# Opening a hybrid decoder block: first four FFN products accumulated side by side, a decay-rate row loaded whole, three small-piece loads issued from GpSimd

## The chip, the core and the metric

The kernel runs on one core of a Trainium2 chip. A core has TensorE (PE in the profile, PEld for its weight loads), VectorE (DVE), ScalarE (ACT), GpSimd (POOL) and SyncE (SP), which work in parallel, each through its own instructions in order, and 16 DMA engines. The metric is the device time of one execution in microseconds (us), lower is better.

## The reference, cut to what matters

One layer of a decoder trunk on 512 tokens of width 1024, all in float32. First comes half a SwiGLU FFN; then three mixing branches (a state-space branch, a dilated attention, a cross-attention); then a second FFN.

```python
def rmsnorm(x, g):
    y = xf * lax.rsqrt(jnp.mean(xf * xf, axis=-1, keepdims=True) + EPS)
    return y * g
def swiglu_ffn(x, w_in, w_down):              # w_in: 1024 x 5632, D_FF = 2816
    a, b = jnp.split(x @ w_in, 2, axis=-1)
    return (jax.nn.silu(a) * b) @ w_down
def s5_scan(u, a_re, a_im, log_dt, b_re, b_im, c_re, c_im, d_skip):
    dt = jnp.exp(log_dt)[:, None]             # 32 groups, 64 states each
    mag = jnp.exp(a_re * dt); ang = a_im * dt # abar = mag * (cos ang, sin ang)
    ...
x = x + 0.5 * swiglu_ffn(rmsnorm(x, ffn1_norm), ffn1_w_in, ffn1_w_down)
u = rmsnorm(x, mix_norm)
...
```

## The kernel before, in words

A tile-level scheduler writes each engine's order of instructions at build time. It simulates the program, takes at each point the ready instruction of highest priority (earliest in the program unless the priority is shifted), and adds the semaphores. On the chip each engine then follows that order: an instruction that waits holds up everything behind it on its engine, and a DMA issue that waits or finds its queue full holds up the later issues of that engine.

**Products.** A float32 product is made of two parts that TensorE takes as fp32r: `split` (lines L124 and L125) writes the rounded part `wh` on ACT and the rest `wl` on DVE, three buffers each. A block of 128 output columns times 512 tokens over 1024 inputs (`mm_T`) is 24 matmuls of 128x512: for each of eight 128-row slices k, `wh` by `uh` (L133), `wh` by `ul` (L134), `wl` by `uh` (L135), all into one PSUM bank of the tag `ps_mm` (four banks). Raw weights come in chunks of 1 MB, 256 columns by 1024 rows, into two buffers `wraw` (L109): a chunk can be loaded when both halves of the chunk that held its buffer have been split.

**The start.** `x` is loaded in four pieces of 256 columns, `xn0` to `xn3` (512 KB each, the first in two halves, L247). TensorE transposes each 128-column slice (L260); ACT and DVE write the split slice `uh`, `ul` scaled by the gain g1 (L139, L140) and an unscaled copy `xT`. GpSimd squares each piece (`sqn`, L270) and DVE reduces it (`ssn`, L271). From the four sums DVE computes `r_nat`, one over the root of the mean square per token (a chain of small `rs_` operations, L149 to L159, L274). `norm_rows` spreads it into the tile `rb`: DVE writes four diagonal tiles `dg` (L231), TensorE multiplies them by ones (L232), DVE copies (L233). As the gain is already in `uh`, `ul`, the row factor is multiplied in behind the product, when PSUM is read (`ff_a`, L297; `ff_b`, L305).

The first two weight chunks of FFN 1, for a and for b, are loaded in four halves of 512 KB (`load_first`, L117), each 128 columns of all 1024 rows: the first behind xn0, the other three behind xn3. Then four products follow one after the other: a of column block 0, b of block 0, a of block 1, b of block 1. Each of them needs all eight slices of x.

**Preparation for the state-space branch** (`ssm_prep`) is written with a lower priority beside FFN 1, so that the scheduler fills gaps with it. It takes `log_dt` (32 numbers, spread over 128 partitions by 16 columns: 2 loads of 1024 single numbers, L410 on SP), computes exp, sine and cosine by small DVE operations (`sm`, L365 to L390), builds tables on GpSimd, and loads `par` (L493), `cn` (L499), `bre` and `bim` (L524, L525: 2048 pieces of 64 bytes each) and `dcol` (L547: 512 single numbers), all on SP. Its tiles come from a pool opened after the pool `start`, which holds xn and sqn, has been closed.

Only the functions around the start, the SSM preparation and FFN 1 are touched.

Of the kernel before, what the change touches and what calls it, by code (L numbers as in the profile page):

```python
# [14 lines left out]
AF = mybir.ActivationFunctionType  # L15
# [69 lines left out]
def kernel(ctx, tc, x, mem, ffn1_norm, ffn1_w_in, ffn1_w_down, mix_norm, w_in, a_re, a_im, log_dt,  # L85
                             b_re, b_im, c_re, c_im, d_skip, w_glu, rel_table, w_up_attn, mem_norm, w_kv, w_up_mem,
                             w_out, ffn2_norm, ffn2_w_in, ffn2_w_down, final_norm, onehot, parity, out):
    nc = tc.nc
    V, S, G, TE = nc.vector, nc.scalar, nc.gpsimd, nc.tensor
# [12 lines left out]
    ident = cpool.tile([P, P], F32, name="ident")  # L102
# [9 lines left out]
    first_raw = {}  # L112
    for c0 in (0, FF):
        first_raw[c0] = wpool.tile([P, KD, 2 * P], F32, name="wraw", tag="wraw", bufs=2)

    def load_first(c0, j):
        nc.sync.dma_start(first_raw[c0][:, :, j * P:(j + 1) * P],  # L117
                          ffn1_w_in[0][:, c0 + j * P:c0 + (j + 1) * P].rearrange("(k p) c -> p k c", p=P))

    def split(raw, eng=V):  # L120
        _, nk, n = raw.shape
        h = wpool.tile([P, nk, n], F32R, name="wh", tag="wh", bufs=3)
        l = wpool.tile([P, nk, n], F32R, name="wl", tag="wl", bufs=3)
        S.activation(h, raw, AF.Copy)  # L124
        eng.tensor_tensor(l, raw, h.bitcast(F32), op=ALU.subtract)  # L125
        return h, l

    def mm_T(ps, w, rhs, first=True, last=True):

        h, l = w  # L130
        n = len(rhs)
        for k in range(n):
            TE.matmul(ps, h[:, k, :], rhs[k][0], start=first and k == 0, stop=False)  # L133
            TE.matmul(ps, h[:, k, :], rhs[k][1], start=False, stop=False)  # L134
            TE.matmul(ps, l[:, k, :], rhs[k][0], start=False, stop=last and k == n - 1)  # L135
# [35 lines left out]
    def ps_tile(tag, bufs=None):  # L171
        return ps["pool"].tile([P, T], F32, name="ps_" + tag, tag="ps_" + tag, bufs=ps["mm"] if tag == "mm" else bufs)
# [6 lines left out]
    g1 = cpool.tile([P, 8], F32, name="g1")  # L179
# [59 lines left out]
    start = ExitStack()  # L239
    sp = start.enter_context(sb_pool("start"))  # L240
    nc.sync.dma_start(g1_in, ffn1_norm[0].rearrange("(k p) -> k p", p=P))
    xn = []
    for c in range(4):
        xc = sp.tile([P, 4, 256], F32, name=f"xn{c}")
        n = 128 if c == 0 else 256
        for h in range(0, 256, n):
            nc.sync.dma_start(xc[:, :, h:h + n], x.rearrange("(j r) d -> j r d", r=4)[:, :, c * 256 + h:c * 256 + h + n])  # L247
        xn.append(xc)
        if c == 0:
            load_first(0, 0)  # L250
    load_first(FF, 0)
    load_first(0, 1)
    load_first(FF, 1)
    pv1 = ps_tile("tr", 2)
    TE.transpose(pv1[:, :8], g1_in, ident[:8, :8])
    V.tensor_copy(g1, pv1[:, :8])
    for k in range(KD):
        pt = ps_tile("mm") if k % 2 or k == 0 else ps_tile("tr", 2)
        for r in range(4):
            TE.transpose(pt[:, r * P:(r + 1) * P], xn[k // 2][:, r, (k % 2) * P:(k % 2 + 1) * P], ident)  # L260
        norm_split(k, pt, g1)
        if k % 2 == 0:
            S.activation(xT[k], pt, AF.Copy)
        else:
            V.tensor_copy(xT[k], pt)
# [11 lines left out]
    U = list(zip(uh, ul))  # L277


    def ffn_in(w, f, pool, g, late_r):  # L280

        if w is ffn1_w_in and f == 0:
            ra, rbk = first_raw[0], first_raw[FF]
        else:
            ra = load_chunk(w[0], 0, KD, f * P, 2 * P)
            rbk = load_chunk(w[0], 0, KD, FF + f * P, 2 * P)
        for j in range(2):
            pa = ps_tile("mm")
            mm_T(pa, split(ra[:, :, j * P:(j + 1) * P]), U)
            if f + j == 0 and late_r:  # L290
                norm_sums()
            pb = ps_tile("mm")
            mm_T(pb, split(rbk[:, :, j * P:(j + 1) * P]), U)
            if f + j == 0:
                norm_rows()
            a = pool.tile([P, T], F32, name="ff_a", tag="ff_a", bufs=2)
            V.tensor_tensor(a, pa, rows["r"], op=ALU.mult)  # L297
            t = pool.tile([P, T], F32, name="ff_t", tag="ff_t", bufs=2)
            S.activation(t, a, AF.Tanh, scale=0.5)
            V.scalar_tensor_tensor(a, t, 1.0, a, op0=ALU.add, op1=ALU.mult)  # L300
            b = pool.tile([P, T], F32, name="ff_b", tag="ff_b", bufs=2)
            if late_r:
                V.tensor_tensor(b, a, pb, op=ALU.mult)  # L303
            else:
                V.tensor_tensor(b, pb, rows["r"], op=ALU.mult)  # L305
                V.tensor_tensor(b, a, b, op=ALU.mult)  # L306
            split_plain(b, *g[f + j])
# [47 lines left out]
    def ssm_prep(pool):  # L355
        cnt = [0]

        def small(dt=F32, shape=(P, 16)):
            cnt[0] += 1
            return pool.tile(list(shape), dt, name=f"sm{cnt[0]}")  # L360
# [44 lines left out]
            return tt(q, exp2i(k2), MUL)  # L405

        are, aim, = vec[:, 32:48], vec[:, 48:64]
        ldt = small()
        for g in range(2):
            nc.sync.dma_start(ldt[64 * g:64 * g + 64, :],  # L410
                                bass.AP(tensor=log_dt.tensor, offset=log_dt.offset + g, ap=[[0, 64], [2, 16]]))
        dt = exp(ldt)
        mag = exp(tt(are, dt, MUL))
        mag2 = tt(mag, mag, MUL)
# [6 lines left out]
        k = round_near(ang, 2.0 / math.pi)  # L421
        r = ang
        for part in PIO2_PARTS:
            r = stt(k, -part, r, MUL, ADD)
        r2 = tt(r, r, MUL)
        q = tsc(r2, 1.0 / math.factorial(9), MUL)
        for n, sg in ((7, -1.0), (5, 1.0), (3, -1.0)):
            q = stt(q, sg / math.factorial(n), r2, ADD, MUL)
        sn = stt(q, 1.0, r, ADD, MUL)
        q = tsc(r2, -1.0 / math.factorial(10), MUL)  # L430
        for n, sg in ((8, 1.0), (6, -1.0), (4, 1.0), (2, -1.0)):
            q = stt(q, sg / math.factorial(n), r2, ADD, MUL)
# [38 lines left out]
        w = 1  # L471
# [23 lines left out]
        for part, src in enumerate((c_re, c_im)):  # L495
            flat = src[0].rearrange("g h p -> (g h) p")
            for i in range(4):
# [6 lines left out]
                pt = ps_tile("tr", 2)  # L504
# [16 lines left out]

        bre = pool.tile([P, 16, 16], F32, name="bre")
        bim = pool.tile([P, 16, 16], F32, name="bim")
        nc.sync.dma_start(bre, b_re[0].rearrange("(q g) p h -> (g p) q h", g=2))  # L524
        nc.sync.dma_start(bim, b_im[0].rearrange("(q g) p h -> (g p) q h", g=2))  # L525
        tmp = pool.tile([P, 16, 16], F32, name="btmp")

        def cscale(b, c, nm):
# [15 lines left out]
            V.memset(dup[part], 0.0)  # L544
        dcol = pool.tile([P, 16], F32, name="dcol")
        V.memset(dcol, 0.0)
        nc.sync.dma_start(dcol[96:, :], d_skip[0].rearrange("(q g) h -> (g h) q", g=2))  # L547
        gs = pool.tile([P, 16, 32], F32, name="gs")
        for i in range(4):
            for part in range(2):  # L550
# [5 lines left out]
                pt = ps_tile("tr", 2)  # L556
# [13 lines left out]
            pt = ps_tile("tr", 2)  # L570
# [617 lines left out]
```

## Time and profile before

| | us |
|---|---|
| median of 3 runs | 1306.02 |
| lowest and highest of the 3 | 1302.16, 1306.84 |
| profiled execution | 1308.34 |
| its span in the trace | 1306.6 |
| TensorE busy | 1266.2 (97%) |
| VectorE busy | 721.0 (55%) |
| ScalarE busy | 417.0 (32%) |
| GpSimd busy | 168.6 (13%) |

The span is what the trace covers of one execution; the 1.7 us between span and profiled time lie around it. A row of the timeline reads: start, time, engine, line, operation, what is written from what, count, and in brackets the idle time before it with what ended it; operations are pipelined, so the start-to-start distance of matmuls is their pace, not the duration. SPq rows are DMA issues on SyncE's queue; their time is that of issuing, not of the transfer. A row of waits reads: who waited for whom, us in total, times, longest. A row of windows reads: stretch, its length, busy time (and instructions) of PE, PEld, DVE, ACT, POOL, granted TensorE clock, DMA share and rate.

### The profile page before, as it was taken

To read this page: it belongs to the slowest core of one execution; us is meant where nothing else is said; L and a number is where in the kernel's file an instruction comes from. 1 tells how busy PE (TensorE), PEld (TensorE's weight loads), DVE (VectorE), ACT (ScalarE), POOL (GpSimd) and SP (SyncE) were. 2 spreads that over 40 slices of the span, in tenths; PEclk is the share of its full clock that TensorE was granted. 3 is DMA by queue.
4 is the path that set the end of the run, shared out by engine and by line. 5 is a ranking of instruction groups with operands and counts; after the bars stand their busy time and mean duration, and the time that the engine had idled before them with its cause. 6 is when DMAs were issued, how large, how long until landed. Compare 5 with 4: busy or idle time off the path is not lost.

```text
span 1306.6 us, 15550 instructions
## 1 busy us (share of the span) xinstructions
PE 1266.2 (97%) x6116; PEld 1039.3 (80%) x6116; DVE 721.0 (55%) x1309; ACT 417.0 (32%) x631; POOL 168.6 (13%) x154
## 2 busy tenths in 40 slices
PE   7598999999999999999999999999999999999997
PEld 5487888778888888998887777888888888888886
DVE  5699555786545847655435555445553444444444
ACT  3222232123323432324433444334233222222223
POOL 2069100440003005230000000001100000000002
PEclk9799999999999999999999999999999999999999
DMA  4421432554525755544217221144423223223231
GB/s 130 114 95 60 166 129 73 138 137 149 167 65 186 234 181 169 164 133 147 81 33 185 65 65 40 61 132 139 129 71 107 95 83 106 91 93 99 95 97 65
DMA packets 161409, 149.34 MB, mean 114 GB/s; under 512 B 34132, under 2 KB 144788, under 8 KB 161044
## 3 DMA queue, kind: packets, MB, share of 16 engines
q1 hardware_dynamic: 137856, 133.75, 33.0%
q10 hardware_dynamic: 23480, 14.59, 3.8%
q8 instruction: 48, 0.79, 0.3%
q14 instruction: 25, 0.20, 0.0%
HBM read 133.35 MB, written 16.16 MB: 114 GB/s over the span
## 4 chain that ended last, share of the span: by engine, by line
PE 87%; DVE 6%; DMA 2%; POOL 2%; SPq 1%; ACT 1%; issue 1%; ACTq 0%; DVEq 0%
PE ps_mm L133 23%; PE ps_mm L135 22%; PE ps_mm L134 22%; PE ps_dn L1096 3%; PE ps_dn L1095 3%; PE ps_dn L1097 3%; DVE wl L125 2%; PE ps_acc L873 1%; PE ps_mm L810 1%; PE ps_mm L811 1%; PE ps_mm L812 1%; PE ps_tr L866 1%; SPq L493 1%; PE ps_acc L721 1%; DMA cn<-in_ssm_c_re_dram 1%
## 5 line engine op out<-in xcount | busy, mean ns | idle before, releaser
L124 ACT ACTIVATE wh<-wraw 128x1024 fp32r<-128x1024 f32 (+2 forms) x238 | 227.6, 958 | 647.5 <-PE ps_mm L134 443.5
L133 PE MATMUL ps_mm<-uh,wh 128*128 128x512 f32 x1056 | 415.3, 394 | 0.5 <-ACT uh L143 0.5
L134 PE MATMUL ps_mm<-ul,wh 128*128 128x512 f32 x1056 | 413.2, 392 | 1.8 <-DVE ul L144 1.8
L135 PE MATMUL ps_mm<-uh,wl 128*128 128x512 f32 x1056 | 414.0, 392 | 0.2 <-DVE wl L125 0.2
L125 DVE TENSOR_TENSOR wl<-wraw,wh 128x1024 fp32r<-128x1024 f32 (+2 forms) x238 | 274.3, 1153 | 176.6 <-ACT wh L124 170.6
L134 PEld LDWEIGHTS ps_mm<-ul,wh 128*128 128x128 f32 x1056 | 199.2, 189 | 43.6 <-DVE ul L144 2.8
L133 PEld LDWEIGHTS ps_mm<-uh,wh 128*128 128x128 f32 x1056 | 199.2, 189 | 42.9 <-ACT uh L143 1.0
L135 PEld LDWEIGHTS ps_mm<-uh,wl 128*128 128x128 f32 x1056 | 199.0, 188 | 43.1 <-issue 0.9
L217 POOL TENSOR_TENSOR sqacc<-sqacc,sqk 128x512 f32<-128x512 f32 x12 | 20.2, 1683 | 476.0 <-ACT sqk L216 476.0
L297 DVE TENSOR_TENSOR ff_a<-ps_mm,rb 128x512 f32<-128x512 f32 x44 | 30.4, 690 | 88.0 <-PE ps_mm L135 87.9
L135 PE MATMUL ps_mm<-gh,wl 128*128 128x512 f32 x176 | 70.6, 403 | 3.3 <-DVE wl L125 3.2
L134 PE MATMUL ps_mm<-gl,wh 128*128 128x512 f32 x176 | 70.7, 402 | 0.0
L133 PE MATMUL ps_mm<-gh,wh 128*128 128x512 f32 x176 | 70.7, 403 | 0.0
L1096 PE MATMUL ps_dn<-wl,gh 128*128 128x512 f32 x176 | 70.2, 399 | 0.0
L1095 PE MATMUL ps_dn<-wh,gh 128*128 128x512 f32 x176 | 69.3, 394 | 0.0
L1097 PE MATMUL ps_dn<-wh,gl 128*128 128x512 f32 x176 | 68.8, 392 | 0.0
L1110 POOL TENSOR_TENSOR x2n<-x2n,fnb 128x512 f32<-128x512 f32 x4 | 5.1, 1296 | 357.1 <-ACT junk L1108 357.1
L303 DVE TENSOR_TENSOR ff_b<-ff_a,ps_mm 128x512 f32<-128x512 f32 x22 | 15.1, 688 | 52.6 <-PE ps_mm L135 52.6
L143 ACT ACTIVATE gh<-ff_b 128x512 fp32r<-128x512 f32 x44 | 27.5, 624 | 50.7 <-DVE ff_b L306 46.3
L135 PEld LDWEIGHTS ps_mm<-gh,wl 128*128 128x128 f32 x176 | 33.4, 190 | 12.5 <-DVE wl L125 4.1
L133 PEld LDWEIGHTS ps_mm<-gh,wh 128*128 128x128 f32 x176 | 33.5, 190 | 8.4 <-issue 0.6
L1095 PEld LDWEIGHTS ps_dn<-wh,gh 128*128 128x128 f32 x176 | 33.0, 188 | 8.6
(318 smaller groups left out, 1663.8 us busy)
## 6 DMA issues: line engine op xcount, KB each, us to landing
wraw<-in_ffn_w_in_dram SPq DMA_DIRECT2D x42, 1024.0 KB, 5.1
wraw<-in_w_in_dram SPq DMA_DIRECT2D x25, 1024.0 KB, 5.4
wraw<-in_ffn_w_down_dram SPq DMA_DIRECT2D x12, 768.0 KB, 4.7
wraw<-in_ffn_w_down_dram SPq DMA_DIRECT2D x8, 1024.0 KB, 5.0
wraw<-in_ffn_w_down_dram SPq DMA_DIRECT2D x10, 512.0 KB, 3.5
wraw<-in_xattn_w_kv_dram SPq DMA_DIRECT2D x4, 1024.0 KB, 6.5
wraw<-in_ssm_w_glu_dram SPq DMA_DIRECT2D x8, 512.0 KB, 7.7
wraw<-in_w_out_dram SPq DMA_DIRECT2D x4, 1024.0 KB, 5.7
```

The costliest lines, as they stand in the source:

```text
L124: S.activation(h, raw, AF.Copy)
L125: eng.tensor_tensor(l, raw, h.bitcast(F32), op=ALU.subtract)
L133: TE.matmul(ps, h[:, k, :], rhs[k][0], start=first and k == 0, stop=False)
L134: TE.matmul(ps, h[:, k, :], rhs[k][1], start=False, stop=False)
L135: TE.matmul(ps, l[:, k, :], rhs[k][0], start=False, stop=last and k == n - 1)
L143: S.activation(h, src, AF.Copy)
L217: (V if k == KD - 1 else G).tensor_tensor(rows["sq"], rows["sq"], sq, op=ALU.add)
L297: V.tensor_tensor(a, pa, rows["r"], op=ALU.mult)
L303: V.tensor_tensor(b, a, pb, op=ALU.mult)
L1095: TE.matmul(pd[r], gh[:, tok], h, start=st, stop=False)
L1096: TE.matmul(pd[r], gh[:, tok], l, start=False, stop=False)
L1097: TE.matmul(pd[r], gl[:, tok], h, start=False, stop=en)
```

## The change

Three edits. First, the first chunks of weights are loaded in eight pieces of 256 KB, each two 128-row slices by 256 columns, two pieces behind each piece of x; and the four first products are accumulated together, in all four `ps_mm` banks: after the two slices of a piece of x are transposed and split, both weight pieces are split and 24 matmuls add those slices to the four products. The transposes get two banks of a new tag `ps_tx` beside the two of `ps_tr`. `ffn_in` at f = 0 then takes the four finished banks. Second, `log_dt` is loaded as one row of 32 numbers repeated on 128 partitions, issued from ACT, and two DVE copies pick the numbers out. Third, the loads of `bre`, `bim` and `dcol` are issued from GpSimd.

```diff
-    def load_first(c0, j):
-        nc.sync.dma_start(first_raw[c0][:, :, j * P:(j + 1) * P],
-                          ffn1_w_in[0][:, c0 + j * P:c0 + (j + 1) * P].rearrange("(k p) c -> p k c", p=P))
+    def load_first(c0, k):
+        nc.sync.dma_start(first_raw[c0][:, k:k + 2, :],
+                          ffn1_w_in[0][k * P:(k + 2) * P, c0:c0 + 2 * P].rearrange("(k p) c -> p k c", p=P))
...
-        if c == 0:
-            load_first(0, 0)
-    load_first(FF, 0)
-    load_first(0, 1)
-    load_first(FF, 1)
+        for c0 in (0, FF):
+            load_first(c0, 2 * c)
...
-    for k in range(KD):
-        pt = ps_tile("mm") if k % 2 or k == 0 else ps_tile("tr", 2)
...
+    first_ps = {(c0, j): ps_tile("mm") for j in range(2) for c0 in (0, FF)}
+    for c in range(4):
+        for k in (2 * c, 2 * c + 1):
+            pt = ps_tile("tx" if k % 2 else "tr", 2)
...
+        for c0 in (0, FF):
+            h, l = split(first_raw[c0][:, 2 * c:2 * c + 2, :])
+            for j in range(2):
+                for i in range(2):
+                    k, cols, o = 2 * c + i, slice(j * P, (j + 1) * P), first_ps[(c0, j)]
+                    TE.matmul(o, h[:, i, cols], uh[k], start=k == 0, stop=False)
+                    TE.matmul(o, h[:, i, cols], ul[k], start=False, stop=False)
+                    TE.matmul(o, l[:, i, cols], uh[k], start=False, stop=k == KD - 1)
...
         for j in range(2):
...
+            if begun:
+                pa, pb = first_ps[(0, j)], first_ps[(FF, j)]
...
-        ldt = small()
+        ldt, ldt_all = small(), small(shape=(P, 32))
+        nc.scalar.dma_start(ldt_all, bass.AP(tensor=log_dt.tensor, offset=log_dt.offset, ap=[[0, P], [1, 32]]))
         for g in range(2):
-            nc.sync.dma_start(ldt[64 * g:64 * g + 64, :],
-                                bass.AP(tensor=log_dt.tensor, offset=log_dt.offset + g, ap=[[0, 64], [2, 16]]))
+            rows = slice(64 * g, 64 * g + 64)
+            V.tensor_copy(ldt[rows], ldt_all[rows].rearrange("p (q g) -> p g q", g=2)[:, g])
...
-        nc.sync.dma_start(bre, b_re[0].rearrange("(q g) p h -> (g p) q h", g=2))
-        nc.sync.dma_start(bim, b_im[0].rearrange("(q g) p h -> (g p) q h", g=2))
+        nc.gpsimd.dma_start(bre, b_re[0].rearrange("(q g) p h -> (g p) q h", g=2))
+        nc.gpsimd.dma_start(bim, b_im[0].rearrange("(q g) p h -> (g p) q h", g=2))
...
-        nc.sync.dma_start(dcol[96:, :], d_skip[0].rearrange("(q g) h -> (g h) q", g=2))
+        nc.gpsimd.dma_start(dcol[96:, :], d_skip[0].rearrange("(q g) h -> (g h) q", g=2))
```

More of the change, by code (lines that the diff above doesn't have):

```diff
@@ L256 @@
     V.tensor_copy(g1, pv1[:, :8])
-    for k in range(KD):
-        pt = ps_tile("mm") if k % 2 or k == 0 else ps_tile("tr", 2)
[L259 to L265, printed above, removed]
+    first_ps = {(c0, j): ps_tile("mm") for j in range(2) for c0 in (0, FF)}
+    for c in range(4):
+        for k in (2 * c, 2 * c + 1):
+            pt = ps_tile("tx" if k % 2 else "tr", 2)
+            for r in range(4):
+                TE.transpose(pt[:, r * P:(r + 1) * P], xn[k // 2][:, r, (k % 2) * P:(k % 2 + 1) * P], ident)
+            norm_split(k, pt, g1)
+            if k % 2 == 0:
+                S.activation(xT[k], pt, AF.Copy)
+            else:
+                V.tensor_copy(xT[k], pt)
+        for c0 in (0, FF):
[6 more added lines that the diff above has]
+                    TE.matmul(o, l[:, i, cols], uh[k], start=False, stop=k == KD - 1)
     ssn = rpool.tile([P, 4, 4], F32, name="ssn")
@@ L280, in ffn_in @@
     def ffn_in(w, f, pool, g, late_r):
-        if w is ffn1_w_in and f == 0:
-            ra, rbk = first_raw[0], first_raw[FF]
-        else:
+        begun = w is ffn1_w_in and f == 0
+        if not begun:
             ra = load_chunk(w[0], 0, KD, f * P, 2 * P)
@@ L287, in ffn_in @@
         for j in range(2):
[L288 to L293, printed above, removed]
+            if begun:
+                pa, pb = first_ps[(0, j)], first_ps[(FF, j)]
+            else:
+                pa = ps_tile("mm")
+                mm_T(pa, split(ra[:, :, j * P:(j + 1) * P]), U)
+                if f + j == 0 and late_r:
+                    norm_sums()
+                pb = ps_tile("mm")
+                mm_T(pb, split(rbk[:, :, j * P:(j + 1) * P]), U)
             if f + j == 0:
```

## The prediction

> **What bounds the kernel now.** I read the page's busy times first, then the waits of TensorE, then busy time by stretches, then the timeline around the largest wait.
>
> ```profile
> span 1306.6 us, 15550 instructions
> PE 1266.2 (97%) x6116; PEld 1039.3 (80%) x6116; DVE 721.0 (55%) x1309; ACT 417.0 (32%) x631; POOL 168.6 (13%) x154
> ...
> PE ps_tr L232 <- DVE dg L231: 14.6, 1, 14.6
> PE ps_tr L260 <- DMA xn<-in_x_dram: 4.3, 1, 4.3
> ...
> 0.00:14.60 14.60, 6.13 (x30) 5.55 (x30) 6.97 (x11) 6.64 (x9) 6.48 (x9) 1.00 0.84 244
> 14.60:31.40 16.80, 16.80 (x79) 13.81 (x77) 10.69 (x19) 6.12 (x9) 2.32 (x2) 1.00 0.19 40
> 31.40:46.30 14.90, 0.30 (x3) 0.01 (x1) 4.02 (x41) 1.06 (x1) 0.00 (x0) 0.61 0.44 92
> 46.30:55.50 9.20, 9.20 (x34) 7.73 (x35) 8.77 (x26) 2.21 (x3) 0.00 (x0) 0.70 0.46 125
> ```
>
> TensorE bounds the kernel (97%), so only its lost time is to be won, and almost all of it lies at the start: no product matmul before 14.6 us, then three products, then 14.6 us of waiting for `dg`, then the fourth product until 55.5. The timeline says why `dg` was late.
>
> ```profile
> 16.91 1.36 SPq L410 DMA_DIRECT2D sm<-in_ssm_log_dt_dram  x2
> 23.45 0.39 SPq L109 DMA_DIRECT2D wraw<-in_ffn_w_in_dram  x1
> 23.88 11.15 SPq L493 DMA_DIRECT2D par<-in_parity_dram  x1
> 24.27 1.02 DVE L544 MEMSET dup<- 128x512 f32 x2
> 40.38 0.18 DVE L367 TENSOR_SCALAR sm<-sm 128x16 f32<-128x16 f32 x1 [14.99 <-DMA sm<-in_ssm_log_dt_dram]
> 44.50 1.06 ACT L124 ACTIVATE wh<-wraw 128x1024 fp32r<-128x1024 f32 x1 [14.16 <-DMA wraw<-in_ffn_w_in_dram]
> 44.84 0.26 DVE L502 TENSOR_SCALAR cd<-cn,par 128x64 f32<-128x64 f32 x1 [1.90 <-DMA cn<-in_ssm_c_re_dram]
> 45.95 0.87 DVE L231 TENSOR_SCALAR dg<-ident,r_nat 128x128 f32<-128x128 f32 x4
> ...
> q1 hardware_dynamic: 653, 0.00, 4.8%
> ```
>
> The last row is the DMA queue from 24 to 30 us: 653 packets, no bytes to speak of, 4.8% of 16 engines. That is `log_dt`, 2,048 single numbers at 6/653 = 9.2 ns each, 18.8 us in all. DVE's order has an operation on it (40.38) ahead of the `rs_` chain, so `r_nat`, `dg` and `norm_rows` wait behind a number that FFN 1 doesn't need. Behind the same pieces stand SP's issue of `par` (11.15 us), the loads of `cn`, and the next weight chunk, issued at 23.45 and landed at 44.5.
>
> **Edit 1: log_dt as one row.** It removes the 2,048 pieces and adds 128 rows of 128 bytes, issued on ACT, and two small DVE copies (an estimate by the 128x16 row above, 0.18 us each). The nearest row for the load is `cn`, also 128 rows, in 1.7 us.
>
> ```profile
> cn<-in_ssm_c_re_dram SPq DMA_DIRECT2D x4, 32.0 KB, 1.7
> bim<-in_ssm_b_im_dram SPq DMA_DIRECT2D x1, 128.0 KB, 8.1
> ...
> q1 hardware_dynamic: 3923, 0.75, 68.8%
> ```
>
> So both stalls go: DVE's 15 us, and SP's queue with what stood in it. What is late next on DVE is `cn`: on SP behind L109, which waits for a split of the first weights (24.7 us by the count below), so `cn` lands near 27 and `dg` is written near 29; needed at 36. ACT's issue stands in ACT's order; what waits behind it are splits that TensorE wants 6 us later. I charge nothing for edit 1's added work; without that cover it is the 1.7 us of a load.
>
> **Edit 2: four products side by side.** I rebuild the start. First the data, from the rows where an engine waited for it.
>
> ```profile
> 4.38 1.97 PE L260 MATMUL ps_mm<-ident,xn 128*128 128x128 f32 x8 [1.67 <-DMA xn<-in_x_dram]
> 9.15 1.06 ACT L124 ACTIVATE wh<-wraw 128x1024 fp32r<-128x1024 f32 x1 [2.08 <-DMA wraw<-in_ffn_w_in_dram]
> 10.68 1.12 PE L260 MATMUL ps_tr<-ident,xn 128*128 128x128 f32 x4 [4.33 <-DMA xn<-in_x_dram]
> 15.49 1.07 ACT L124 ACTIVATE wh<-wraw 128x1024 fp32r<-128x1024 f32 x1 [0.19 <-DMA wraw<-in_ffn_w_in_dram]
> 14.60 0.48 PE L133 MATMUL ps_mm<-uh,wh 128*128 128x512 f32 x1
> 16.98 0.60 PE L260 MATMUL ps_tr<-ident,xn 128*128 128x128 f32 x4
> 54.36 0.39 PE L134 MATMUL ps_mm<-ul,wh 128*128 128x512 f32 x1
> 55.26 0.39 PE L135 MATMUL ps_mm<-uh,wl 128*128 128x512 f32 x1
> 47.30 0.43 PE ps_mm L133
> 52.22 0.23 PE ps_mm L133
> ```
>
> In order of issue, 1.0 MB was there at 9.15, 1.5 MB at 10.7, 3.0 MB at 15.5: 3.2 us per MB. In the new order the first weight piece ends at 0.75 MB, so 8.3 us; the second at 9.15; then x and weights of the four steps are complete at 9.15, 12.3, 15.5 and 18.7. With 0.6 us for the first split (a little over half of the 1.06 row) the first product matmul starts at 9.0 instead of 14.6.
>
> One step is 24 matmuls; the pace is (55.26 - 54.36)/4 = 0.225 us, so 5.4 us. Transposes of the next two slices: four in 0.60 us, so 1.2 per step. A step takes 6.6 us, twice the 3.2 us of its data. Its other engines keep up, by these rows:
>
> ```profile
> L140 DVE SCALAR_TENSOR_TENSOR ul<-ps_mm,g,uh 128x512 fp32r<-128x512 f32 x5 | 3.7, 746 | 3.4 <-ACT uh L139 3.3
> L265 DVE COPY xT<-ps_mm 128x512 f32<-128x512 f32 x4 | 2.7, 681 | 0.0
> L144 DVE TENSOR_TENSOR gl<-ff_b,gh 128x512 fp32r<-128x512 f32 x1 | 0.7, 681 | 0.0
> L271 DVE TENSOR_REDUCE ssn<-sqn 128x4 f32<-128x1024 f32 x4 | 4.8, 1212 | 0.0
> L297 DVE TENSOR_TENSOR ff_a<-ps_mm,rb 128x512 f32<-128x512 f32 x2 | 1.4, 681 | 0.0
> L232 PE MATMUL ps_tr<-dg,ones 128*128 128x128 f32 x8 | 2.3, 440 | 14.6 <-DVE dg L231 14.6
> ```
>
> DVE per step: two `ul` (1.5), one `xT` (0.7), two half-size `wl` (1.4, as `gl`), one `ssn` (1.2), together 4.8 us, less than 6.6. ACT has less still.
>
> The clock at the start: the windows show 1.00, but transposes at 10.68 took 1.12 us for four, at 16.98 only 0.60, and after the long idle the matmuls ran 0.43 us apart from 47.3 until 52 and then 0.23. So TensorE worked at half pace for the 3.9 us from 10.68 to 14.6, and for some 5.5 us after 46.3. The new first step meets this with matmuls instead of transposes: 3.9 to 5.5 us at half pace lose 2.0 to 2.8; I take 2.3, and 0 as the other end, should the early transposes already have set the pace. The Trainium skill, "TensorE: Matmul & The Clock Gate", Part 1, has the idle clock at half and releases it after about 3.4 us of activity; taken alone it would cost 1.7 us here, and it agrees with the pace in these rows and not with the granted clock of 1.00 beside them.
>
> End of the fourth product: 9.0 + 5.4 + 2.3 + 3 x 6.6 = 36.5 us. All four banks are then full, and the next chunk's product needs one: `norm_rows` (8 passes, 2.3 us at half pace, so some 1.0), the copy to `rb` (0.7) and `ff_a` (0.7) come first, 2.4 us; 0 if the scheduler put `norm_rows` earlier. Then 38.9, against 55.6 for the same point before (the fourth product's last matmul at 55.26, and two transposes behind it). **Gain 16.7 us.** The next chunk's weights are not late: their buffer is free when the last a-piece is split, which waits for a `wh` buffer that step 2 gives back at 23.3; split by 24.7, landed 5 us later.
>
> **Edit 3: bre, bim, dcol from GpSimd.** 4,096 pieces of 64 bytes and 512 of 4 leave SP's queue. No GpSimd load is in this trace, so I bound it. Floor: 40 to 46 us moved 3,923 packets at 68.8% of the engines, 1.5 ns a piece, 7 us for all. Ceiling: `log_dt`'s 9.2 ns a piece, 42 us. GpSimd's own rows:
>
> ```profile
> 5.31 1.90 POOL L270 TENSOR_TENSOR sqn<-xn 128x1024 f32<-128x1024 f32 x1 [4.02 <-DMA xn<-in_x_dram]
> 10.70 6.22 POOL L270 TENSOR_TENSOR sqn<-xn 128x1024 f32<-128x1024 f32 x3 [3.50 <-DMA xn<-in_x_dram]
> ...
> POOL cosT L477 <- DVE sm L372: 59.0, 1, 59.0
> ```
>
> Its last `sqn` ends at 16.9 and it then has nothing to do for 59 us, which hides either, provided that the issues stand behind the four `sqn`. I take it that they do: DVE had idle time before 10 us, yet the preparation's first operations (`dup`, 24.27) ran only when x was used up. The floor is nearest, since it is the same loads; cost nothing on the path, 7 us of DMA between 19 and 27 us, where only one 1 MB chunk with 6 us to spare runs.
>
> The Trainium skill, "DMA: Bandwidth & Descriptors", section "Issuing engines are not separate DMA queues", speaks against expecting more of this edit: loads from all engines share the same 16 DMA engines and interleave. No run here shows a GpSimd load; if the loads went out at the start, its rule would give the first rival.
>
> **Behind the start** the preparation overloads DVE and GpSimd:
>
> ```profile
> 126.00:135.00 9.00, 5.82 (x19) 4.37 (x18) 9.00 (x6) 1.48 (x2) 8.24 (x4) 0.81 0.57 188
> ```
>
> TensorE loses 3.2 us there and 0.19 x 9 = 1.7 to the clock. The preparation and FFN 1 both move ahead by about the same time, so I leave it; it can vanish (-5) or grow (+5).
>
> **The sum.** Against the profiled execution: 1308.3 - 16.7 = 1291.6. Its time is 2.3 above the median of 1306.0; against that 1289.3.
>
> **The rivals.**
> - *Early small pieces* (0.15). GpSimd is idle until 5.3 us; if the issues stand ahead of `sqn`, 4,608 pieces take up to 7 us of all DMA engines beside x and the first weights: 1296. For it: nothing that the code orders; against it: the late `dup`.
> - *Another head of line* (0.10). DVE still meets `cn` or the new row late, `rb` misses 36.5 and TensorE idles and cools: 5 to 9 us, so 1294 to 1299.
> - *Given back* (0.08). The scheduler's new order makes the jam at 126 worse, or adds one; twice that jam and a cold restart return some 10 us: 1299 to 1303, within the bound of no change.
> - *Slower* (0.06). One mechanism: GpSimd makes the pieces slowly and ahead of `sqn`. DVE's `ssn` then waits, and behind it the splits that TensorE needs for step 2. The restart is at X + 3, X being GpSimd's hold (one `sqn` and one `ssn`, 1.9 + 1.2), the same point is reached at X + 3 + 19.8 + 2.4; that passes 55.6 from X = 30 us on. At the ceiling of 42 it is 67, a loss of 12: 1318.
> - *It does not do what it says* (0.01): the row lands as late as the pieces; then only the earlier start counts, about 1300.
>
> **How the numbers follow.** The main case has 0.60: 1289.3, own range 1281 (no `norm_rows` wait, -2.4; jam gone, -4.9) to 1295 (jam grows, +5). For 8 in 10 the range reaches from 1280 over the first two rivals to 1299. Half a per cent, 6.5 us, is about what a measurement tells from no change (the three runs spread 4.7). Faster, below 1299.5: 0.60 + 0.15 + 0.09 of the rest = 0.84; same 0.09; slower 0.07.
>
> **What would show it.** Right: first product matmul near 9, matmul pace 0.43 then 0.225, no wait of `dg` over 3 us, the f = 2 products starting near 39, SP's issue of `par` under 1 us. Wrong: `sqn` or `ssn` waiting behind GpSimd's issues; a DVE wait for `cn` or the row past 36 us; the time before the f = 2 products won, and lost again between 60 and 140 us.

## The result, and the profile after

The changed kernel takes 1295.38 us (median; 1293.01 to 1295.93) beside 1306.24 for the kernel before in the same session: a ratio of 0.992, 95% interval 0.9896 to 0.9944. Five more rounds on another chip gave 1293.42 against 1304.86, 0.9915 (0.9901 to 0.993). So it is faster by some 11 us. One execution of a kernel told below, r_row, ran at a granted clock of 0.77 and took 1527.33 us; its ratio leaves that one out. The forecast was 1289.3 with a range of 1280 to 1299: the direction and the range held, and the likeliest value was 6 us too low.

First the head of the page after, and TensorE's waits. A row of waits reads: who waited for whom, us in total, times, longest.

```profile
span 1293.4 us, 15577 instructions
PE 1265.6 (98%) x6116; PEld 1038.5 (80%) x6116; DVE 727.0 (56%) x1315; ACT 417.5 (32%) x635; POOL 169.9 (13%) x157
PE ps_mm L135 <- DVE wl L125: 7.1, 3, 3.8
```

The 14.6 us wait for `dg` is gone and no other has taken its place at the start. On top now stands a wait of the down products (the second half of FFN 1, with `w_down`) for `wl`, 7.1 us in three pieces. In the kernel before the same row read 3.4:

```profile
PE ps_mm L135 <- DVE wl L125: 3.4, 2, 3.2
```

Now the timeline of the start after (start, us, engine, line, what is written from what, count; in brackets the idle time before it).

```profile
8.87 1.22 PE L271 MATMUL ps_mm<-uh,wh 128*128 128x512 f32 x2 [2.60 <-ACT wh L124]
12.88 0.63 PE L272 MATMUL ps_mm<-ul,wh 128*128 128x512 f32 x1
13.30 0.63 PE L271 MATMUL ps_mm<-uh,wh 128*128 128x512 f32 x1
16.35 0.39 PE L271 MATMUL ps_mm<-uh,wh 128*128 128x512 f32 x1
16.58 0.39 PE L272 MATMUL ps_mm<-ul,wh 128*128 128x512 f32 x1
18.30 1.35 POOL L535 DMA_DIRECT2D bre<-in_ssm_b_re_dram  x1
19.65 1.16 POOL L536 DMA_DIRECT2D bim<-in_ssm_b_im_dram  x1
29.35 0.57 SPq L504 DMA_DIRECT2D par<-in_parity_dram  x1
30.91 0.07 DVE L479 MEMSET cosT<- 128x16 f32 x1 [0.84 <-PE ps_tx L260]
31.46 0.38 ACTq L419 DMA_DIRECT2D sm<-in_ssm_log_dt_dram  x1
33.42 1.05 PE L232 MATMUL ps_tr<-dg,ones 128*128 128x128 f32 x8
37.85 0.50 PE L133 MATMUL ps_mm<-uh,wh 128*128 128x512 f32 x1 [0.27 <-DVE ff_a L307]
```

The reader is to see four things. The first product matmul runs at 8.87, and matmuls start 0.42 us apart at 13 and 0.23 apart at 16.4. The transposes by `dg` (`norm_rows`, 33.42) run inside the fourth step, so the second chunk's products (f = 2) start at 37.85 with 0.27 us of waiting. SyncE's issue of `par` fell from 11.15 us to 0.57. And `log_dt` is asked for only at 31.46, just after the memset at 30.91 that had to wait for the last transposes of x.

The place where time was given back is shown by windows of 5 us (stretch, its length, busy time and instructions of PE, PEld, DVE, ACT, POOL, granted clock, DMA share, GB/s).

```profile
105.00:110.00 5.00, 3.70 (x17) 2.68 (x16) 4.96 (x5) 1.36 (x2) 5.00 (x6) 1.00 0.00 0
110.00:115.00 5.00, 3.85 (x17) 2.77 (x15) 4.96 (x5) 0.00 (x0) 5.00 (x4) 1.00 0.51 157
115.00:120.00 5.00, 4.08 (x12) 3.18 (x13) 4.99 (x4) 1.79 (x3) 4.92 (x4) 0.69 0.01 3
120.00:125.00 5.00, 1.92 (x8) 1.25 (x6) 4.97 (x4) 1.15 (x2) 4.84 (x3) 0.97 0.39 159
125.00:130.00 5.00, 4.31 (x13) 3.45 (x14) 5.00 (x5) 0.00 (x0) 2.88 (x1) 0.71 0.77 267
```

TensorE is busy 17.9 of these 25 us, so it idles 7.1, the wait above; DVE is full in all five windows and GpSimd nearly to its last operation. Two stretches also show a granted clock of 0.69 and 0.71: there matmuls start 0.43 us apart instead of 0.23. Before, the same jam (the stretch in which the down products' splits come late) was shorter: 3.2 us idle between 126 and 135.

To measure it in one number for every kernel I take the distance from the first f = 2 matmul to the row of the fourth sum of a down product (`xT`, behind the jam; each sum adds a down product to `xT`). The work between is 361 matmuls in every kernel but x4_dup and r_dup. After, it ends here; the second row is that of before, which started f = 2 at 55.63:

```profile
131.27 0.69 DVE L599 SCALAR_TENSOR_TENSOR xT<-ps_mm,xT 128x512 f32<-128x512 f32 x1 [1.11 <-PE ps_mm L135]
143.88 0.69 DVE L588 SCALAR_TENSOR_TENSOR xT<-ps_mm,xT 128x512 f32<-128x512 f32 x1 [2.28 <-PE ps_mm L135]
```

That is 93.4 us after and 88.25 before. The balance of the two profiled executions: 17.8 us won up to f = 2, 5.2 lost from there to the fourth sum, 0.6 won in the whole rest, together 13.2, which is the difference of the spans (1306.6 and 1293.4). A second profile of the changed kernel (r_after) gives 19.4 won, 8.4 lost, 1.8 won.

The window over the distance says what it is made of; after's reads:

```profile
37.85:131.27 93.42, 86.28 (x361) 69.92 (x362) 89.17 (x231) 24.49 (x33) 56.66 (x66) 0.96 0.30 101
```

TensorE idles 7.1 us of it and is busy 86.3. Without a wait and at full clock it is busy 82.4 for the same matmuls (x5_notab below), so the other 3.9 go to matmuls at half clock. Before had 3.5 us idle and 2.4 at half clock: of the 5.2 us lost, 3.7 are waits and 1.5 the clock.

### The profile page after: what moved, and what is told of

Its sections match the earlier page's. It is cut to its first block, busy times and chain, and to the rows that moved or that the text cites. A ratio compares the mean times of both kernels' runs of the same rounds, so it can differ in the third digit from the quotient of the medians.

```text
span 1293.4 us, 15577 instructions
## 1 busy us (share of the span) xinstructions
PE 1265.6 (98%) x6116; PEld 1038.5 (80%) x6116; DVE 727.0 (56%) x1315; ACT 417.5 (32%) x635; POOL 169.9 (13%) x157
## 4 chain that ended last, share of the span: by engine, by line
PE 86%; DVE 4%; DMA 4%; POOL 4%; ACT 1%; issue 1%; SPq 0%; ACTq 0%; POOLq 0%; DVEq 0%
PE ps_mm L133 22%; PE ps_mm L135 22%; PE ps_mm L134 22%; PE ps_dn L1107 3%; PE ps_dn L1106 3%; PE ps_dn L1108 3%; DMA cad<-ca 2%; DVE wl L125 1%; PE ps_acc L884 1%; PE ps_mm L821 1%; PE ps_mm L823 1%; PE ps_mm L822 1%; PE ps_tr L877 1%; DMA wraw<-in_ffn_w_in_dram 1%; PE ps_acc L732 1%
## 5 line engine op out<-in xcount | busy, mean ns | idle before, releaser
L133 PE MATMUL ps_mm<-uh,wh 128*128 128x512 f32 x1024 | 402.0, 393 | 0.8 <-ACT uh L143 0.6
L134 PE MATMUL ps_mm<-ul,wh 128*128 128x512 f32 x1024 | 399.8, 391 | 1.6 <-DVE ul L144 1.6
L135 PE MATMUL ps_mm<-uh,wl 128*128 128x512 f32 x1024 | 400.3, 391 | 0.0
L125 DVE TENSOR_TENSOR wl<-wraw,wh 128x1024 fp32r<-128x1024 f32 (+2 forms) x242 | 277.3, 1147 | 176.7 <-ACT wh L124 170.6
L133 PEld LDWEIGHTS ps_mm<-uh,wh 128*128 128x128 f32 x1024 | 192.7, 188 | 42.0 <-ACT uh L143 1.0
L134 PEld LDWEIGHTS ps_mm<-ul,wh 128*128 128x128 f32 x1024 | 192.7, 188 | 41.6 <-DVE ul L144 1.9
L135 PEld LDWEIGHTS ps_mm<-uh,wl 128*128 128x128 f32 x1024 | 192.5, 188 | 41.4 <-issue 0.9
L134 PEld LDWEIGHTS ps_mm<-gl,wh 128*128 128x128 f32 x176 | 33.9, 193 | 8.1 <-issue 0.2
```

## The experiments

The experiments tell two explanations apart. **A**: the gain is that of the `log_dt` row; the four products and the GpSimd loads add little at the start, and the longer jam is a consequence of edit 2, which keeps x in use until 30 us and so delays the preparation against FFN 1. **B**: all three edits carry the gain, and the jam grew because DVE got more work or by chance of the new order. One row of the table is one profiled execution; the medians are of the timed runs, and each ratio is to the kernel before in the same session. The last two columns split what the distance has over 82.4 us: TensorE idle, and TensorE busy longer (half clock; in x4_dup and r_dup also nine and four matmuls more, 2.0 and 0.9 us, that ran before the row).

| kernel | median us | ratio to before (95%) | f = 2 starts | first table op | fourth sum | distance | idle | busy longer |
|---|---|---|---|---|---|---|---|---|
| before | 1306.24 | 1 | 55.63 | 75.91 | 143.88 | 88.25 | 3.5 | 2.4 |
| after | 1295.38 | 0.992 (0.9896 to 0.9944) | 37.85 | 69.98 | 131.27 | 93.4 | 7.1 | 3.9 |
| x1_row | 1292.38 | 0.9892 (0.9868 to 0.9916) | 38.90 | 59.39 | 128.57 | 89.7 | 4.0 | 3.3 |
| x2_four | 1311.62 | 1.0042 (1.0029 to 1.0055) | 54.13 | 88.70 | 149.88 | 95.75 | 6.7 | 6.6 |
| x3_sp | 1296.93 | 0.9925 (0.9897 to 0.9953) | 38.60 | 72.33 | 136.07 | 97.5 | 10.8 | 4.2 |
| x4_dup | 1286.76 | 0.9858 (0.9829 to 0.9888) | 37.09 | 69.24 | 126.13 | 89.0 | 2.6 | 4.0 |
| x5_notab | 1281.67 | 0.9813 (0.9799 to 0.9828) | 36.88 | 69.02 | 119.29 | 82.4 | 0 | 0 |
| x6_row_dup | 1291.39 | 0.9884 (0.9868 to 0.9901) | 39.85 | 60.33 | 127.34 | 87.5 | 2.8 | 2.3 |
| x7_trfirst | 1292.39 | 0.9898 (0.9882 to 0.9913) | 40.18 | 60.75 | 129.04 | 88.9 | 4.3 | 2.2 |
| x8_trfirst_dup | 1292.51 | 0.99 (0.9879 to 0.9921) | 39.53 | 61.30 | 128.57 | 89.0 | 3.0 | 3.6 |
| r_after | 1293.42 | 0.9915 (0.9901 to 0.993) | 36.22 | 68.38 | 132.92 | 96.7 | 7.7 | 6.6 |
| r_row | 1291.3 | 0.9893 (0.9878 to 0.9908) | 39.36 | 59.85 | 129.16 | 89.8 | 4.0 | 3.4 |
| r_dup | 1287.61 | 0.9867 (0.9853 to 0.988) | 35.98 | 68.09 | 124.95 | 89.0 | 2.6 | 3.9 |
| x9_late | 1288.88 | 0.9883 (0.9864 to 0.9901) | 37.72 | 69.86 | 120.14 | 82.4 | 0 | 0 |

"First table op" is GpSimd's first operation on the table `cosT`. What lies behind the fourth sum takes 1158.5 to 1164.5 us in these profiled executions whatever the edit; no difference of total time under some 3 us between two kernels is laid to a cause here on the strength of one profile.

### x1_row: before, with log_dt as one row alone

```diff
 # before.py
-            nc.sync.dma_start(ldt[64 * g:64 * g + 64, :], ...)      # single numbers
+        nc.scalar.dma_start(ldt_all, ... ap=[[0, P], [1, 32]])
+            V.tensor_copy(ldt[rows], ldt_all[rows].rearrange("p (q g) -> p g q", g=2)[:, g])
```

> The kernel before with edit 1 alone (log_dt as one row from ACT; products, loads and queues as before). Theory A: the row alone takes away both the wait for dg and the full queue of SP, so the fourth product follows the third without a gap (31.4 + 5.4 us) and the f = 2 products start at 37 to 39 us, as in the changed kernel; then edit 2's earlier start (8.9 instead of 14.6 us) is worth nothing, since the transposes and the half-paced clock only move in between the matmuls. Median 1294 to 1298. Theory B, the prediction's sum: the 5.7 us of earlier start are a part of the gain of their own; f = 2 starts at 42 to 44 and the median is 1299 to 1302.

Measured: 1292.38 us, 0.9892 (0.9868 to 0.9916). The timeline of this kernel:

```profile
17.44 0.39 ACTq L409 DMA_DIRECT2D sm<-in_ssm_log_dt_dram  x1
38.90 0.48 PE L133 MATMUL ps_mm<-uh,wh 128*128 128x512 f32 x1
59.39 0.23 POOL L478 TENSOR_TENSOR cosT<-cosT,sm 128x16 f32<-128x16 f32 x1 [42.32 <-DVE sm L372]
```

The row alone brings f = 2 to 38.90, only 1.05 us behind the full change. It asks for `log_dt` 14 us earlier than after does, its tables start 10.6 us earlier, and its jam is about as before (89.7). It is the whole gain; B falls in its first half. Theory A had f = 2 right and the median 2 us too high.

### x2_four: after, with edits 1 and 3 undone

```diff
 # after.py
-        nc.scalar.dma_start(ldt_all, ...)
-            V.tensor_copy(ldt[rows], ...)
+            nc.sync.dma_start(ldt[64 * g:64 * g + 64, :], ...)      # single numbers
-        nc.gpsimd.dma_start(bre, ...)      # bim, dcol likewise
+        nc.sync.dma_start(bre, ...)
```

> The changed kernel with edits 1 and 3 undone (four products side by side, log_dt as 2,048 single numbers on SP, bre, bim and dcol on SP). Theory A: DVE's order still has an operation on log_dt ahead of the rs_ chain, so rb comes after 40 us, TensorE waits and cools, f = 2 starts at 46 to 52; median 1300 to 1306. Theory B: four banks full of work cover most of the wait, f = 2 starts near 43 and the median is 1296 to 1300.

Measured: 1311.62 us, 1.0042 (1.0029 to 1.0055): slower than before, and than both theories said. Its first wait and its timeline:

```profile
PE ps_tr L515 <- DVE rb L233: 17.0, 1, 17.0
28.42 2.03 SPq L420 DMA_DIRECT2D sm<-in_ssm_log_dt_dram  x2
32.05 1.05 PE L232 MATMUL ps_tr<-dg,ones 128*128 128x128 f32 x8
51.20 0.17 DVE L377 TENSOR_SCALAR sm<-sm 128x16 f32<-128x16 f32 x1 [17.27 <-DMA sm<-in_ssm_log_dt_dram]
52.20 0.68 DVE L233 COPY rb<-ps_tr 128x512 f32<-128x512 f32 x1
54.13 0.79 PE L133 MATMUL ps_mm<-uh,wh 128*128 128x512 f32 x1 [0.20 <-DVE ff_a L307]
```

The old stall is only moved one operation on: `dg` and `norm_rows` are done by 33.1, but the copy to `rb` stands behind the preparation's operation on `log_dt`, which waits 17.27 us. The pieces are asked for 11.5 us later than before (28.42, before 16.91), so they land later (51.2, before 40.4). The earlier first product wins 1.5 us at f = 2, and the distance is 7.5 longer than before: 3.2 more idle and 4.2 more at half clock. Most of the latter is no jam: behind the 17 us wait the f = 2 matmuls start 0.43 us apart from 54.1 to 59.8.

### x3_sp: after, with edit 3 undone

```diff
 # after.py
-        nc.gpsimd.dma_start(bre, ...)      # bim, dcol likewise
+        nc.sync.dma_start(bre, ...)
```

> The changed kernel with edit 3 undone (bre, bim, dcol on SP). Theory A: the queue that was full was full of log_dt, so edit 3 is worth nothing: 1293 to 1298, f = 2 start at 38 within 1 us. Rival: bim's issue (5.2 us on SP before) and the small pieces hold up the chunks for f = 2, 1298 to 1302.

Measured: 1296.93 us, 0.9925 (0.9897 to 0.9953), which cannot be told from after. Its profiled execution, 1301.36 us, is 4.4 over its median. In that trace f = 2 starts 0.75 us later and the jam is longer:

```profile
PE ps_mm L135 <- DVE wl L125: 10.8, 3, 7.5
PE ps_tr L516 <- DVE rb L233: 2.1, 1, 2.1
```

The second row stands just before f = 2: DVE waits 1.8 us for the `log_dt` row (its copy is at 35.94), and `rb` comes behind it. TensorE idles, and the f = 2 matmuls then start 0.43 us apart until 41.7, which loses 1.7 more. So without edit 3 this execution lost about 2.4 us at the start. One profile and overlapping intervals settle neither that nor whether GpSimd's loads help the jam; the distance, 97.5, is hardly over r_after's 96.7.

### x4_dup and r_dup: after, with the 64 dup copies on ACT

```diff
 # after.py, L566
-                        V.tensor_copy(du[pr, :, 3 - k, g, :], bb[k][part][pr, 4 * i:4 * i + 4, :])
+                        S.activation(du[pr, :, 3 - k, g, :], bb[k][part][pr, 4 * i:4 * i + 4, :], AF.Copy)
```

> The changed kernel with the 64 copies dup <- bb (14.5 us of DVE between 60 and 135 us) moved from DVE to ACT. Theory C: of the 17.7 us won at the f = 2 start, 4.5 are given back between 100 and 131 us because DVE, slowed by GpSimd's tables, can't split weights fast enough; with the copies gone TensorE's waits for wl (7.1 us) shrink to under 2 us and the median falls to 1286 to 1291. Rival D: the length of GpSimd's table chain sets the end of the jam, or ACT's order now waits for GpSimd before it splits: wl waits stay over 5 us, median 1293 to 1300.

> The changed kernel with the 64 dup copies on ACT instead of DVE, once more. Theory (the jam behind the start is DVE beside a busy GpSimd): 1286 to 1289, 6 to 9 us under the changed kernel on the same chip. Rival (the earlier difference was order noise of the rest of the kernel and the chip's): within 3 us of the changed kernel.

Measured: 1286.76 us, 0.9858 (0.9829 to 0.9888), and on the other chip 1287.61, 0.9867 (0.9853 to 0.988), 5.8 under after there, a little less than the 6 to 9 expected. This is the fastest version with an unchanged output: on that chip it is also 3.7 us under the row alone (r_row, 1291.3), and no execution of either reaches the other's. `dup` are 64 small copies of `bb` that the preparation makes. First the groups of `dup` and of the `wl` splits between 60 and 135 us in after, then `dup` and the `wl` wait in x4_dup (busy us, mean ns of one, idle before):

```profile
L566 DVE COPY dup<-bb 64x64 f32<-64x64 f32 x16 | 14.5, 904 | 0.8 <-POOL bb L544 0.7
L125 DVE TENSOR_TENSOR wl<-wraw,wh 128x768 fp32r<-128x768 f32 x7 | 12.3, 1760 | 0.0
```

```profile
L566 ACT ACTIVATE dup<-bb 64x64 f32<-64x64 f32 x16 | 4.1, 254 | 17.6 <-POOL bb L547 9.0 <-POOL bb L544 8.5
PE ps_mm L135 <- DVE wl L125: 1.9, 1, 1.9
```

Sixteen copies of 64 by 64 take DVE 14.5 us in this stretch and ACT 4.1. With them off DVE the wait falls from 7.1 to 1.9 and the distance from 93.4 to 89.0. In the pair on one chip the distance falls by 7.7 (96.7 to 89.0), which is the whole difference of the spans (1293.8 and 1286.1).

### x5_notab: after, with the last two doublings of the tables left out

The output of this kernel is not the reference's: where the table is doubled to 64 and 128 columns, two ACT copies stand for the six GpSimd operations.

```diff
 # after.py, L488 to L493
+            if w < 32:
                 G.tensor_tensor(cosT[:, :, hi], cosT[:, :, lo], cb, op=MUL)
                 ...
+            else:
+                S.activation(cosT[:, :, hi], cosT[:, :, lo], AF.Copy)
+                S.activation(sinT[:, :, hi], sinT[:, :, lo], AF.Copy)
```

> The changed kernel, leaving out the last two doublings of the cosine and sine tables on GpSimd (12 operations of 1 to 3 us, 24 us of GpSimd at 99 to 128 us; ACT copies the lower half instead, so the tables hold wrong values). DVE's own work is unchanged. Theory C1: the jam is DVE made slow by GpSimd beside it: wl 128x768 falls from a mean of 1.76 us to under 1.2, the copies dup from 0.90 to under 0.5, TensorE's waits for wl from 7.1 us to under 2 us, median 1286 to 1290. Rival C2: DVE has too much work of its own there; the waits stay over 5 us, median 1293 to 1297.

Measured: 1281.67 us, 0.9813 (0.9799 to 0.9828). No wait for `wl` is left among TensorE's waits, and the same two groups between 60 and 135 us read, with the window over the distance behind them:

```profile
L125 DVE TENSOR_TENSOR wl<-wraw,wh 128x768 fp32r<-128x768 f32 x8 | 8.1, 1013 | 0.1
L570 DVE COPY dup<-bb 64x64 f32<-64x64 f32 x16 | 7.3, 456 | 0.8 <-POOL bb L548 0.7
36.88:119.29 82.41, 82.41 (x361) 67.84 (x362) 74.97 (x231) 27.77 (x37) 34.66 (x54) 1.00 0.36 121
```

DVE does each `wl` split in 1.01 us instead of 1.76, and the same copies in half the time, when GpSimd has no large operation beside them. The distance is 82.4, TensorE busy throughout at a granted clock of 1.00: this is the stretch without a jam. The median is 4 us under what theory C1 said. Before had therefore lost 5.9 us here, after 11.0.

How the two engines hold each other up can be read off after's timeline at 118 us.

```profile
118.10 4.25 DVE L566 COPY dup<-bb 64x64 f32<-64x64 f32 x2
122.98 0.68 DVE L599 SCALAR_TENSOR_TENSOR xT<-ps_mm,xT 128x512 f32<-128x512 f32 x1
119.90 2.39 POOL L490 TENSOR_TENSOR cosT<-cosT,tab_tmp 128x1024 f32<-128x1024 f32 x1
122.37 2.46 POOL L492 TENSOR_TENSOR tab_tmp<-cosT,sm 128x1024 f32<-128x1024 f32 x1
```

The two copies (0.18 us each at their fastest in this trace) take 1.89 and 2.35 us. The second ends at 122.35, when GpSimd's operation that began at 119.90 ends (122.29). They took turns with whole GpSimd operations. The `xT` sum, which reads PSUM, takes 0.68 in the same stretch as elsewhere, and copies of the same size on ACT took 0.25. The Trainium skill, "SBUF — State Buffer", section "SBUF: two separate sides", gives this as a rule: DVE and GpSimd share one pair of ports as an exclusive lock held for a whole instruction, where the DVE operation reads two SBUF inputs or runs in its two-port mode, and ACT never waits for it. The rows agree, except that none shows in which mode a copy runs; the small 64 by 64 copies are the costliest by this rule, as each can wait for an operation over ten times its length (2.39 us beside 0.18).

### x7_trfirst: after, with all transposes written ahead of the four products

```diff
 # after.py, behind the copies to xT (L265)
+    for c in range(4):
         for c0 in (0, FF):
             h, l = split(first_raw[c0][:, 2 * c:2 * c + 2, :])
```

> The changed kernel with all transposes of x written ahead of the four products, so that the scheduler lets them pass when their data is there; loads, four products and queues as in the changed kernel. Theory E: edit 2 holds x and with it the pool of the preparation until 30 us, so log_dt is asked for at 31 and not at 17 us, GpSimd's tables begin 32 us behind the f = 2 products instead of 20, and meet the down products. Then here the first operation on log_dt comes at 22 to 28 us, the first table operation at 58 to 63, the fourth sum of the first down products at 126 to 129 (131.3 in the changed kernel), median 1287 to 1292. Rival F: the place of the preparation doesn't matter, the four banks emptied at once make the jam: median 1294 to 1297.

Measured: 1292.39 us, 0.9898 (0.9882 to 0.9913). Now x is used up earlier, and the preparation with it:

```profile
26.08 0.14 DVE L423 COPY sm<-sm 64x16 f32<-64x16 f32 x1
PE ps_mm L135 <- DVE wl L125: 4.3, 3, 2.0
```

The row is copied at 26.08 (after: 35.20), the tables start 20.6 us behind f = 2 (after: 32.1; before and x1_row: 20.3 and 20.5), and the distance falls to 88.9, as before. In the jam itself TensorE idles 4.3 us (after: 7.1), and none of it is at half clock (granted clock 1.00 from 65 to 150 us). So the longer jam comes from how late the preparation stands against FFN 1, which edit 2 sets by keeping x in use. The total wins 1 to 3 us only, as f = 2 starts 2.3 us later: here TensorE waits 3.0 us before it for `cd`, `rb` and `vec`, which DVE writes late, and the first f = 2 matmuls run at half pace until 42.9. The median lies at the upper edge of theory E, below rival F.

### x6_row_dup and x8_trfirst_dup: both remedies at once

x6_row_dup is x1_row, x8_trfirst_dup is x7_trfirst, each with the `dup` line of x4_dup.

> The kernel before with edit 1 alone and the copies dup on ACT. If the jam behind the start is what is left, it falls from the 1292.4 us of edit 1 alone by what x4_dup gained on the changed kernel or less, as its waits for wl were 4.4 us and not 7.1: 1285 to 1289. Rival (the gain came from the four products' order): 1291 to 1294.

> x7_trfirst with the copies dup on ACT as well: both causes of the jam taken away. Theory E and C together: 1283 to 1287, the fastest of all; if they take away the same loss, no better than x4_dup, 1286 to 1288.

Measured: 1291.39 us, 0.9884 (0.9868 to 0.9901), and 1292.51 us, 0.99 (0.9879 to 0.9921). The first lies in its rival's range, the second above both of its ranges. The two remedies don't add, and the traces say why.

Where the tables are early, the copies have less to win: TensorE idles 4.0 us in x1_row's distance and 4.3 in x7_trfirst's, against 7.1 and 7.7 in the changed kernel. Moving the copies takes some 3 us of waits for `wl` away, but TensorE then waits for `wh`, the split that ACT makes beside the copies: 1.9 us in x6_row_dup and 1.6 in x8_trfirst_dup, where x1_row and x7_trfirst have no such wait. So the idle time falls by 1.3 us only; in the changed kernel it falls by 4.5 and 5.1. And x8_trfirst_dup starts like x7_trfirst: 3.2 us of waits before f = 2, then half pace until 44.8, which is its 3.6 us of longer busy time.

### r_after and r_row: the changed kernel and the row alone, once more

> The changed kernel once more, beside the next three on one chip. Expected 1295 (1293 to 1296), ratio to before 0.990 to 0.994. It is the base for the differences to the three others.

> Before with log_dt as one row alone, once more. Theory (edit 1 holds the whole gain; what edits 2 and 3 win at the start they lose in the jam behind it): 1290 to 1293, that is 2 to 5 us under the changed kernel on the same chip. Rival (the changed kernel is the better one and the earlier difference was the chip's): 1296 or more, over the changed kernel.

Measured side by side on one chip: 1293.42 us, 0.9915 (0.9901 to 0.993), and 1291.3 us, 0.9893 (0.9878 to 0.9908). The row alone is 2.1 us under the full change; the intervals overlap by a little. Edits 2 and 3 together are worth nothing beside the row, and perhaps less, as long as `dup` is on DVE. With it on ACT they seem to be worth 2 to 4 us (ratios 0.9858 and 0.9867 of x4_dup and r_dup, 0.9884 of x6_row_dup), but the intervals overlap and no session has both. The distance of r_after is 96.7, again far over r_row's 89.8.

### x9_late: x4_dup, with the last two doublings moved into the third stage

```diff
 # x4_dup
-        while w < P:                    # all seven doublings here
+        double(32)                      # five here
 ...
+        yield                           # resumed in the third stage
+        double(P)
+        for s, tb in enumerate((cosT, sinT)):
+            nc.scalar.dma_start(csd[s], tb.rearrange("p g t -> p (g t)"))
```

> The same with the dup copies on ACT, and the last two doublings of the tables (GpSimd, 128x512 and 128x1024) moved out of FFN 1 into the third stage of the state-space branch, near 290 us, with the stores of the tables behind them; the output is unchanged. Theory (the last doublings beside the splits of the down products are what holds DVE): no wait of TensorE for wl before 140 us, the fourth down sum near 120 instead of 126, and 1280 to 1284, as with the doublings left out, 1281.7. Rival (moved work costs the same where it goes): the fourth down sum near 120 as well, but 1286 to 1290, with DVE slowed and TensorE waiting for wl between 285 and 330 us.

Measured: 1288.88 us, 0.9883 (0.9864 to 0.9901), beside 1287.61 for r_dup. The jam is gone as with the doublings left out (fourth sum at 120.14, distance 82.4), and no time is won. GpSimd did ten of the twelve operations at 255 to 275 us (two stayed near 100 us), and there TensorE waits three times; the longest in x9_late's timeline:

```profile
266.02 0.63 PE L573 MATMUL ps_tr<-ident,dup 128*128 128x128 f32 x4 [1.95 <-DVE gs L588]
```

Windows of r_dup and, behind them, x9_late:

```profile
240.00:270.00 30.00, 28.37 (x174) 22.32 (x173) 16.42 (x26) 11.63 (x39) 14.65 (x11) 1.00 0.55 144
270.00:280.00 10.00, 10.00 (x46) 8.18 (x45) 7.62 (x14) 4.16 (x6) 0.00 (x0) 1.00 0.39 128
```

```profile
240.00:270.00 30.00, 26.99 (x164) 21.15 (x165) 18.59 (x25) 11.57 (x39) 26.72 (x19) 1.00 0.54 141
270.00:280.00 10.00, 8.61 (x39) 6.78 (x38) 9.61 (x14) 3.28 (x4) 4.92 (x2) 1.00 0.60 220
```

TensorE idles 4.4 us of these 40 against 1.6, and DVE is busy 28.2 us against 24.0 for about as many operations. x9_late was 4.8 us ahead at the fourth sum (3.9 without the four matmuls more before r_dup's row) and is 1.5 ahead at the end, so it lost 2.4 to 3.3 us in between, which these 2.8 fit. So the theory held for the place that the work leaves, and the rival for the total; the place that it named, a wait for `wl` after 285 us, was wrong.

## Why the prediction was right, and where it was off

**Edit 1: right, and it is the whole gain.** Both stalls went, as said; `dg` was no longer waited for. With the row alone f = 2 starts at 38.90. What I credited to edit 2, the rebuilt start, is nearly all the removal of the stall.

**The first product at 9.0, half pace costing 2.3: right.** It ran at 8.87, at half pace until 14.4, so 5.5 us and a loss of 2.8, the upper end of the bounds. The other end, no loss, is excluded. The Trainium skill, "TensorE: Matmul & The Clock Gate", Part 1, releases the clock after about 3.4 us of activity; here matmuls that began at 8.87 were still at half pace 4.9 us later (the last pair at that distance starts at 13.3 and 13.7), with a granted clock of 1.00 in the record; the measured pace decides.

**The fourth product at 36.5 and then 2.4 us of waiting: the sum right, its parts not.** `norm_rows` ran inside the last step at 33.42 (the other end that I kept), so the wait was 0.27; in return the four products end about 1 us later than reckoned. f = 2 at 37.85 instead of 38.9, a gain of 17.8 instead of 16.7.

**What edit 2 wins by itself: not asked.** The forecast compared the new start with the old one, stall and all. Against x1_row the first product is 5.4 us earlier (14.30 there), and f = 2 only 1.05. The windows of the half-paced stretch, after first and x1_row behind it:

```profile
8.80:14.40 5.60, 5.53 (x14) 4.26 (x15) 5.55 (x7) 2.23 (x5) 2.86 (x2) 1.00 1.05 347
```

```profile
8.80:14.40 5.60, 3.61 (x21) 3.56 (x22) 3.94 (x4) 3.67 (x6) 3.58 (x2) 1.00 1.12 319
```

x1_row idles 2.0 us here, after 0.1; with the 0.2 that stand between them later, the gain is 2.1. But x1_row also has only 3.6 busy us at half pace instead of 5.5, which loses it half of 1.9 less, 1.0. What remains is 1.1. The rest of the 5.4 us x1_row spends on transposes that the changed kernel does later, among its products.

**Edit 3: nothing on the path, right; both bounds on its loads too high.** The two issues took GpSimd 1.35 and 1.16 us, behind the squares, and the loads landed in under 5 us, where SyncE's took 7.0 and 8.1 before (6.4 and 6.5 in x3_sp). Both were there 5.6 us after the first issue, less than the floor of 7:

```profile
bre<-in_ssm_b_re_dram POOLq DMA_DIRECT2D x1, 128.0 KB, 4.8
bim<-in_ssm_b_im_dram POOLq DMA_DIRECT2D x1, 128.0 KB, 4.2
q0 software_dynamic: 128, 0.26, 0.2%
```

**"Behind the start ... I leave it": this term failed.** Its premise was that the preparation and FFN 1 move ahead by about the same time. FFN 1 moved 17.8 us; the tables moved 5.9:

```profile
75.91 0.23 POOL L477 TENSOR_TENSOR cosT<-cosT,sm 128x16 f32<-128x16 f32 x1 [58.99 <-DVE sm L372]
69.98 0.23 POOL L488 TENSOR_TENSOR cosT<-cosT,sm 128x16 f32<-128x16 f32 x1 [36.92 <-DVE sm L382]
```

The page before had what was needed: the preparation's tiles come from a pool opened when x is used up, and edit 2 keeps x in use until its fourth step. By my own count the last transposes stand behind the third step, 9.0 + 5.4 + 2.3 + 2 x 6.6 = 29.9 us, instead of 17 before. So the large table operations fell later against the down products' splits, and the term was not 0 but +5.2 us (3.7 of waits, 1.5 of half clock), and +8.4 in r_after's profile, past the +5 that I had kept as its bound. I had named this loss as what would make the forecast wrong; I gave its place no sum.

**The size of the miss.** For the profiled execution I forecast 1291.6 and it took 1295.22: 5.2 for the jam, less 1.1 for the better start and 0.6 for the rest. The other 2.5 of the 6.1 us to the median are my allowance for the profiled execution of before, 2.3 above its median; the one of after stands at its median.

The rivals of another head of line, of early pieces and of slow pieces from GpSimd did not occur in the changed kernel; the first shows in x7_trfirst and x3_sp, where TensorE waits 3.0 and 2.4 us just before f = 2 and then runs at half pace. "Given back" is half true: 5.2 of its 10 us.

## What to carry to other kernels

Before crediting a rebuilt stage with the time of a stall, price the smallest edit that takes away the stall alone: here a new load of one row gave all that three edits gave. What the rebuilt stage is worth can depend on a loss further on: the four products seem to show in the time only once the copies are off DVE. When two streams of work share engines, give each one's shift a sum of its own; who moves ahead by how much decides what falls beside what. Work off the path is not free when it makes another engine's operations wait: here copies that seem tiny were the ones to move off DVE while GpSimd ran long operations.

## What the runs showed of the hardware that I had not expected

- DVE beside a busy GpSimd: a `wl` split of 128x768 takes 1.01 us on average without the large table operations and 1.76 beside them, a 64x64 copy 0.18 at best and 0.90 on average beside them, while the sums that read PSUM keep their time (0.68).
- 4,096 pieces of 64 bytes issued from GpSimd in two loads stand in the record, together with the 512 single numbers of `dcol`, as 128 packets, and each of the two lands in 4.2 to 4.8 us; from SyncE they took 6.4 to 8.1.
- Behind waits of TensorE of 2 us and more just before f = 2, the next matmuls started 0.43 us apart instead of 0.23 for 2.7 to 5.7 us (x7_trfirst, x3_sp, x8_trfirst_dup, x2_four).
- Work moved some 150 us later met other DVE operations, which took longer beside it, and TensorE idled 2.8 us more there.
